# The attention's end and the output projection of layer 1 in program order on TensorE

## The chip, the cores and the metric

The kernel runs on one core of one Trainium2 chip. The metric is the device time of one execution in microseconds (us), the median of several runs, lower is better. The engines are named as the profile names them: PE (TensorE matmul), PEld (its weight load), DVE (VectorE), ACT (ScalarE), POOL (GpSimd), SP (SyncE, which issues transfers).

## The reference

One inference step of a decoder trunk with two layers over 1024 prompt tokens and 8 sample tokens, all in float32, with D_MODEL = 1024 and D_FF = 4096. Layer 0 mixes tokens by a recurrent block, layer 1 by attention with a window of 128 tokens, 16 heads of 64 and 4 KV heads. Each mixer and each MLP is added to the residual stream. The part that matters here is layer 1's mixer; the sample tokens attend to a cache:

```python
def swa_sample(x, k_cache, v_cache, w_qkv, q_g, k_g, sinks, w_out):
    q, k, v = qkv_heads(x, w_qkv, q_g, k_g)
    k_all = jnp.concatenate([k_cache, k], axis=1)
    v_all = jnp.concatenate([v_cache, v], axis=1)
    ...
    o = sink_attention(q, k_all, v_all, dist, mask, sinks)
    y = o.reshape(n, s, Q_DIM) @ w_out
    return y, k_all[:, s:], v_all[:, s:]
```

The prompt's heads go through the same `sink_attention` in blocks of 128, and through the same `w_out`. Behind it follows `h = h + y`, an RMS norm, and the MLP.

## The kernel before

Activations lie as 8 tiles of 128 features by 1032 tokens (1024 of the prompt, then 8 sample tokens). The tokens are cut into 3 chunks c of 344, so the sample tokens stand in chunk 2. A float32 product is made of three: both operands are split into a high and a low part (`oh`, `ol` and `wh`, `wl`), and oh·wh, ol·wh and oh·wl are summed.

**The output projection of layer 1** (`entry_steps`, lines 395 to 430) has a group for each c and each of 8 output tiles m: 8 steps over the features with 3 products 128x344 each, 24 "long products" (line 244). For m < 4 and c < 2, six of the eight steps are done early, while the attention still runs, and the last two later. Behind a group DVE adds the residual tile (L418), ACT issues the write to DRAM (L419), squares (L290) and scales (L421). A generator yields behind every three products, so that the caller can put other work there. When group m = 4 of a chunk is reached (m = 5 for c = 1), `factors` makes the norm's block sums of the chunk before: ACT casts the sum of squares (`shi`, L278), DVE makes the rest (`slo`, L279), and PE multiplies both by ones (L280, L281).

**The attention** runs over 32 steps g. Each has three stages: scores of a step two ahead (`stage_a`, L1033), transposes (`stage_b`, L1060) and values (`stage_c`, L1080, for two steps together). `order` says at which step and in which place of it the scores of step g are written. Between them stand steps of a filler: the query projections up to g = 22 (G0), the early part of the output projection from there on.

**The samples' chain** (`samples`, lines 1115 to 1163) is a generator too: a square on ACT (L1117), a sum over features on PE (L1119), 16 score products of 8 columns (L1131), a copy, a transpose on PE (L1136), a softmax on DVE and ACT (L1138 to L1145), a transpose on PE (L1147), 16 value products of 8 columns (L1154, "short products" as those of L1131), and copies by DVE (L1157, L1163) into the columns that chunk 2 needs. `load_cache` issues its transfers on SP. `between(m, c)` is called ahead of each group, starts both, and asks for weights and residual tiles (`need`).

**The order of the work.** The engines each run their own stream in order. A scheduler makes these streams from the program's order and from estimates. `pinned()` ties the PE instructions inside it to program order, by a dependence from each to the next. The attention's steps stand inside it. The last `stage_c` and the loop that drains the filler, which runs the greater part of the output projection, stand outside:

```python
for _ in fill:
    for s in side:
        next(s, None)
```

Here the scheduler places the samples' products and the block sums among the long products by itself. With each product on 128x128 weights goes a weight load, which PE runs beside the product ahead.

Of the kernel before, what the change touches and what calls it, by code (L numbers as in the profile page):

```python
# [26 lines left out]
NB = SEQ // P  # L27
# [38 lines left out]
def trunk(ctx: ExitStack, tc: tile.TileContext, I, O):  # L66
# [51 lines left out]
    def B(tag=None):  # L118
        if tag is None:
            tag = ring[turn[0] % len(ring)]  # L120
            turn[0] += 1
        return psum["pool"].tile([P, 512], F32, tag=tag, bufs=BANKS[tag], name=nm("b" + tag))
# [71 lines left out]
    for o in [("x", m) for m in range(4)] + LRU:  # L194
        if o[0] == "g":
            units.append(("gate", o[1], I["w_gate"][o[1]], W))
        elif o[0] in "xo":
            m = o[1] + (8 if o[0] == "x" else 0)
# [630 lines left out]
    def attention(hs):  # L829
# [181 lines left out]
        @contextmanager  # L1011
        def pinned():
            block = tc.nc.cur_bb.bb
            n = len(block.instructions)
            yield
            seq = [i for i in block.instructions[n:] if i.engine == pe.engine]
            for x, y in zip(([last["pe"]] if "pe" in last else []) + seq, seq[0 if "pe" in last else 1:]):
                tc.add_manual_dep(y, x.name, mybir.DependencyInfo(mybir.DependencyClass.NoSync, mybir.DependencyReason.DATA), reason="pinned")
            if seq:
                last["pe"] = seq[-1]  # L1020
# [74 lines left out]
        def load_cache():  # L1095
            z = S("z")
            sp.dma_start(z[:, 129:257], I["dist_s"])
            zs.append(z)
            for p in range(2):
                kt = A("kc")  # L1100
                kv = kt[:, :D].rearrange("p (n j) -> p n j", n=NS)
                sp.dma_start(kv[:, :, 0:127], I["k_cache"][p])
                dve.tensor_copy(kv[:, :, 127], ks[:, p, :])
                sp.dma_start(O["ks"][p], kt[:, :D])
                kc.append(kv)
            for h in range(2):
                vt = A("vc")
                vv = vt[:, :D].rearrange("p (n j) -> p n j", n=4)
                for part in (slice(0, 112), slice(112, 127)):
                    sp.dma_start(vv[part], I["v_cache"][part, 4 * h:4 * h + 4, :])  # L1110
                sp.dma_start(vt[127:128, :D], vnew[h:h + 1, :])
                sp.dma_start(O["vs"][h], vt[:, :D])
                vc.append(vv)

        def samples():
            sb = S("ssb")
            act.activation(sb[:, :P], qrow, AF.Square, scale=4.0)  # L1117
            st = B("N")
            pe.matmul(st[:, 0:1], lhsT=sb[:, :P], rhs=ones[:, 0:1], start=True, stop=True)  # L1119
            r = S("r")[:, :1]  # L1120
            rstd_m2(st[:, 0:1], r, 1)
            dve.tensor_scalar(dd[:, 2:3], r, 0.0625, None, ALU.mult)
            dve.reciprocal(dd[:, 3:4], dd[:, 2:3])
            dve.tensor_tensor(dd[:, 3:4], dd[:, 3:4], V("slope_row"), ALU.mult)
            dve.tensor_scalar(qrow, qrow, V("qg"), None, ALU.mult)
            yield
            st = B("N")
            for n in range(NS):
                for p in range(2):
                    o = n * 16 + p * 8  # L1130
                    pe.matmul(st[:, o:o + 8], lhsT=kc[p][:, n, :], rhs=qblk[:, n, p, :, :].rearrange("p u i -> p (u i)"),  # L1131
                              start=True, stop=True)
                    yield
            dve.tensor_copy(sb[:, :P], st[:, :P])
            st2 = B("N")
            pe.transpose(st2[:, :P], sb[:, :P], ident)  # L1136
            z = zs[0]
            dve.tensor_scalar(z[:, 129:257], z[:, 129:257], dd[:, 3:4], -1.0, ALU.mult, ALU.mult)  # L1138
            dve.tensor_copy(z[:, 128:129], nsink_row)
            dve.tensor_tensor_reduce(z[:, 0:P], st2[:, :P], z[:, 129:257], scale=dd[:, 2:3], scalar=nsink_row[:, 0:1],  # L1140
                                     op0=ALU.add, op1=ALU.min, accum_out=dd[:, 0:1])
            e = S("e")
            act.activation(e[:, 0:P + 1], z[:, 0:P + 1], AF.Exp, scale=-1.0, bias=dd[:, 0:1], accum_out=dd[:, 1:2])
            dve.reciprocal(dd[:, 1:2], dd[:, 1:2])
            dve.tensor_scalar(e[:, 0:P], e[:, 0:P], dd[:, 1:2], None, ALU.mult)  # L1145
            st3 = B("N")
            pe.transpose(st3[:, :P], e[:, :P], ident)  # L1147
            dve.tensor_copy(sb[:, P:2 * P], st3[:, :P])
            yield from range(8)
            st4 = B("N")  # L1150
            for n in range(NS):
                for p in range(2):
                    o = n * 16 + p * 8
                    pe.matmul(st4[:, o:o + 8], lhsT=vc[n // 4][:, n % 4, p * P:p * P + P], rhs=sb[:, P + o:P + o + 8],  # L1154
                              start=True, stop=True)
                    yield
            dve.tensor_copy(sb[:, :P], st4[:, :P])  # L1157
            sv = sb[:, :P].rearrange("p (n q u i) -> p n q u i", n=NS, q=2, u=2)
            for t in range(8):
                p, i = divmod(t, 4)  # L1160
                for u in range(2):
                    h = slice(64 * u, 64 * u + 64)
                    dve.tensor_copy(osm[h, t, :], sv[h, :, p, u, i])  # L1163
# [23 lines left out]
        def between(m, c):  # L1187
            if (m, c) == (0, 0):
                swap_banks("po")
            if c < 0 or (m, c) == (4, 0):  # L1190
                need(m + 1)
            if m >= 4 and c == 0:
                need(min(m + 2, M8))
            if (m, c) == (6, 0):
                load_cache()
            if (m, c) == (7, 0):
                side.append(samples())
            if (m, c) == (0, 2):
                for t in range(8):
                    split_act_dve(ohl[t][0], ohl[t][1], osm[:, t, :], slice(SEQ, T))  # L1200

        side = []
        fill = filler()

        NG = 4 * NB
# [5 lines left out]
        def upto(n):  # L1211
            take(n - taken[0])

        def pace(table, g):
            at = max((k for k in table if k <= g), default=min(table))
            to = min((k for k in table if k > g), default=at)
            return table[at] if to == at else table[at] + (table[to] - table[at]) * max(0, g - at) / (to - at)
# [21 lines left out]
        order = {}  # L1239
        for g in range(AHEAD, NG):  # L1240
            at = g - AHEAD
            place = {25: (23, 3), 26: (24, 1)}.get(g) or (at, {0: 3, 1: 1}.get(g % NB, 0))
            order[place] = g

        for g in range(NG):
            table = FILL if g < G0 else EARLY

            def scores(place):
                if (g, place) in order:
                    ready(order[g, place])  # L1250
                    run(stage_a(order[g, place]))

            with pinned():
                scores(0)
                if g != G0:
                    upto(int(pace(table, g + 1 / 3)))
                if g and g % 2 == 0:
                    stage_c(g - 2)
                if g == G0:
                    run(fill)  # L1260
                    taken[0], fill = 0, steps
                scores(1)
                upto(int(pace(table, g + 2 / 3)))
                run(stage_b(g))
                upto(int(pace(table, g + 1)))
                scores(3)
            if g == 17:
                for t in (4, 5):
                    ohl[t] = (A("oh"), A("ol"))
            if g in (20, 21, 23, 24):  # L1270
                ensure(index["wo1", (20, 21, 23, 24).index(g)])
            if g == G0 - 1:
                for t in range(4):
                    load_o(t, cs(0))
                for t in (6, 7):
                    ohl[t] = (A("oh"), A("ol"))
                srcs = [ohl[t] for t in range(8)]
                r1 = A("rt")
                rs["r1"] = r1
                xs, need, steps = out_proj("wo1", srcs, spill, "g_mlp1", r1, spill1, before=between, after=ahead(1),  # L1280
                                          early=(4, 5, 0, 1, 2, 3))
                for t in range(4):
                    load_o(t, cs(1))
            if g == 26:
                for t in range(4):
                    load_o(t, slice(2 * CH, SEQ))
        stage_c(NG - 2)

        for _ in fill:
            for s in side:  # L1290
                next(s, None)
        return xs


# [345 lines left out]
```

## Time and profile before

| | |
|---|---|
| time, median of 3 runs | 1960.44 us (1960.01 to 1960.88) |
| the profiled execution's own time | 1958.56 us |
| its span | 1956.8 us |
| PE busy | 1944.1 us, 99% |
| DVE, ACT, POOL busy | 1480.5, 1007.9, 370.1 us |
| mean granted PE clock | 0.998 |

The span is the time from the first to the last instruction. The profile lists groups of instructions by source line, what each engine waited for, windows of the span with the busy time of each engine and the granted clock, and a timeline. A row of the timeline has the start, the duration, engine, line, operation, output and inputs, and in brackets the idle time ahead of it with what ended it. The long products follow each other closer than their duration says, since they are pipelined: what one costs is the distance from start to start.

### The profile page before, as it was taken

The page shows a single profiled execution, that of the slowest core. Times are in us where ns is not written, and L with a number is a line of the kernel's source. Part 1 is how long each engine was busy: PE and PEld are TensorE (multiplying, and loading weights), DVE is VectorE, ACT ScalarE, POOL GpSimd, SP SyncE. Part 2 cuts the span into 40 slices and gives each one's busy share as a digit, 9 for nine tenths or more (in the row PEclk, how much of TensorE's full clock was granted, in tenths as well). Part 3 has the DMA queues.
Part 4 walks back from the last instruction along what each step waited for, and adds up shares of the span by engine and source line. Part 5 has one row for each costly group of instructions (what it writes and reads, how often), then busy time and mean ns, then how long its engine had stood idle before and what let it go on. Part 6 is the DMA issues. An engine that isn't in the chain of part 4 may idle for free.

```text
span 1956.8 us, 34219 instructions
## 1 busy us (share of the span) xinstructions
PE 1944.1 (99%) x12844; PEld 1808.8 (92%) x12844; DVE 1480.5 (76%) x2712; ACT 1007.9 (52%) x1993; POOL 370.1 (19%) x702
## 2 busy tenths in 40 slices
PE   9999999999999999999999999999999999999998
PEld 8999999999999899999999887999999999999998
DVE  8896737987777888778753778579877779687884
ACT  6476635543434655455553667555443436455552
POOL 2330000000000232322022667000000003223221
PEclk9999999999999999999999999999999999999999
DMA  5111242244445788888453446622443447788876
GB/s 184 44 44 54 67 170 83 109 152 157 141 157 172 232 224 239 215 197 210 135 152 87 111 110 195 212 72 105 157 145 138 162 167 261 212 197 217 237 193 181
DMA packets 115909, 308.17 MB, mean 157 GB/s; under 512 B 17560, under 2 KB 46240, under 8 KB 115744
## 3 DMA queue, kind: packets, MB, share of 16 engines
q0 software_dynamic: 30720, 104.18, 22.0%
q1 hardware_dynamic: 54496, 129.36, 20.1%
q10 hardware_dynamic: 30528, 72.45, 10.3%
q8 instruction: 101, 1.65, 0.4%
q14 instruction: 64, 0.52, 0.1%
HBM read 178.08 MB, written 115.16 MB: 150 GB/s over the span
## 4 chain that ended last, share of the span: by engine, by line
PE 91%; DVE 3%; issue 2%; ACT 2%; DMA 1%; POOL 1%; SPq 0%; ACTq 0%; DVEq 0%; POOLq 0%
PE bD L609 35%; PE bZ L609 26%; PE bP L244 11%; PE bS L244 7%; PE bT L244 3%; PE bP L939 3%; PE bO L1080 1%; PE bSS L1033 1%; PE bS L969 1%; PE bT L1060 1%; ACT se L1046 1%; DMA x<-xT 0%; DVE wl L184 0%; DVE hl L1323 0%; DVE sq L295 0%
## 5 line engine op out<-in xcount | busy, mean ns | idle before, releaser
L609 PEld LDWEIGHTS bD<-op,op 128*128 128x128 f32 x3072 | 380.6, 188 | 7.9
L609 PE MATMUL bD<-op,op 128*128 128x260 f32 x3072 | 383.1, 282 | 0.0
L609 PEld LDWEIGHTS bD<-tl,op 128*128 128x128 f32 x2880 | 362.3, 188 | 11.7 <-DVE ho L757 0.3
L609 PE MATMUL bD<-tl,op 128*128 128x260 f32 x2880 | 366.5, 282 | 0.1
L622 POOL DMA_DIRECT2D tl<-hsum x210 | 125.2, 681 | 889.7 <-PE bD L609 786.5
L456 ACT CAST op<-ws 128x512 fp32r<-128x512 f32 (+2 forms) x288 | 158.6, 560 | 245.5 <-DVE ws L577 119.9
L609 PE MATMUL bZ<-op,op 128*128 128x512 f32 x1152 | 282.3, 395 | 0.0
L609 PE MATMUL bZ<-tl,op 128*128 128x512 f32 x1080 | 271.9, 395 | 1.0 <-ACT he L731 0.8
L609 PEld LDWEIGHTS bZ<-op,op 128*128 128x128 f32 x1152 | 210.4, 188 | 43.8 <-ACT he L743 0.4
L609 PEld LDWEIGHTS bZ<-tl,op 128*128 128x128 f32 x1080 | 194.3, 188 | 38.7 <-ACT he L731 1.0
L464 DVE TENSOR_TENSOR tl<-tl 128x520 fp32r<-128x520 f32 (+1 forms) x210 | 136.7, 692 | 77.2 <-ACT tl L463 77.1
L456 ACT CAST op<-raw 128x512 fp32r<-128x512 f32 (+2 forms) x216 | 120.9, 561 | 135.8 <-PE bD L609 73.6
L457 DVE TENSOR_TENSOR op<-ws,op 128x512 fp32r<-128x512 f32 (+2 forms) x288 | 171.4, 610 | 7.3 <-ACT op L456 7.1
L457 DVE TENSOR_TENSOR op<-raw,op 128x512 fp32r<-128x512 f32 (+2 forms) x216 | 131.6, 610 | 10.6 <-ACT op L456 9.8
L757 DVE TENSOR_TENSOR ho<-bD,ho 128x520 f32<-128x520 f32 x140 | 97.5, 696 | 36.8 <-PE bD L609 35.9
L463 ACT CAST tl<-tl 128x520 fp32r<-128x520 f32 (+1 forms) x210 | 117.7, 626 | 3.0 <-DMA tl<-hsum 1.5
L184 DVE TENSOR_TENSOR wl<-raw,wh 128x512 fp32r<-128x512 f32 (+1 forms) x73 | 63.8, 891 | 34.4 <-ACT wh L183 17.7
L747 DVE TENSOR_TENSOR ho<-bZ,ho 128x512 f32<-128x512 f32 x72 | 49.5, 688 | 43.6 <-PE bZ L609 43.3
L731 ACT COPY he<-bZ 128x512 f32<-128x512 f32 x72 | 42.0, 583 | 74.9 <-PE bZ L609 67.9
L757 DVE TENSOR_TENSOR he<-bD,he 128x520 f32<-128x520 f32 x71 | 49.4, 696 | 40.6 <-PE bD L609 40.3
L749 ACT COPY he<-bZ 128x512 f32<-128x512 f32 x68 | 39.9, 587 | 77.0 <-PE bZ L609 65.0
L183 ACT CAST wh<-raw 128x512 fp32r<-128x512 f32 (+1 forms) x76 | 57.1, 775 | 32.1 <-PE bT L244 11.3
(372 smaller groups left out, 3833.4 us busy)
## 6 DMA issues: line engine op xcount, KB each, us to landing
raw<-w_up SPq DMA_DIRECT2D x64, 512.0 KB, 3.9
tl<-hsum POOLq DMA_DIRECT2D x120, 260.0 KB, 6.8
raw<-w_dn SPq DMA_DIRECT2D x64, 384.0 KB, 6.4
tl<-hsum POOLq DMA_DIRECT2D x90, 256.0 KB, 6.5
spill<-ho POOLq DMA_DIRECT2D x32, 516.0 KB, 6.8
spill<-he POOLq DMA_DIRECT2D x32, 516.0 KB, 6.5
hsum<-ts ACTq DMA_DIRECT2D x30, 520.0 KB, 4.0
hsum<-ho ACTq DMA_DIRECT2D x30, 516.0 KB, 3.6
```

What stands on the lines that cost most here:

```text
L183: act.copy(r_(hi[:, sl]), raw[:, sl])
L184: eng.tensor_tensor(r_(lo[:, sl]), raw[:, sl], hi[:, sl], ALU.subtract)
L244: pe.matmul(o, lhsT=r_(wt[:, col(k):col(k) + P]), rhs=r_(xt[:, cs(c)]), start=(k == first and a == 0), stop=(k == final and a == 2))
L456: act.copy(r_(hi), x)
L457: dve.tensor_tensor(r_(lo), x, hi, ALU.subtract)
L463: act.copy(r_(hi), lo)
L464: eng.tensor_tensor(r_(lo), lo, hi, ALU.subtract)
L609: pe.matmul(d[:, 512 * b:512 * b + c], lhsT=r_(wt[:, j * P:j * P + P]), rhs=r_(xt[:, c * b:c * b + c]), start=first and j == 0 and a == 0, ...
L622: pool.dma_start(t[:, n:2 * n], src)
L747: dve.tensor_tensor(o0, d, o[:, HP], ALU.add)
L757: last["sum"] = dve.tensor_tensor(t, inner(d), t, ALU.add).ins
L939: pe.matmul(o, lhsT=r_(wt[:, k * P:k * P + P]), rhs=r_(xt[:, cs(c)]), start=(k == 0 and a == 0), stop=(k == M8 - 1 and a == 2))
```

## The change

1. The last `stage_c` and the draining loop stand inside `pinned()`. PE so runs the whole output projection of layer 1, with the samples' products and the block sums, in program order.
2. In `samples`, three filler steps are yielded ahead of the first transpose and nine ahead of the second, and three instead of eight ahead of the value products.
3. `load_cache` is called at (m, c) = (3, 0) instead of (6, 0), and `samples` starts at (6, 0) instead of (7, 0). An assertion says that the samples are done when (0, 2) is reached.
4. The scores of steps 17 and 18 get other places in `order`.
5. At g = 22 two steps of the output projection (six long products) stand ahead of `stage_c`, where there were none.

```diff
--- before.py
+++ after.py
@@ -1132,6 +1132,7 @@
                               start=True, stop=True)
                     yield
             dve.tensor_copy(sb[:, :P], st[:, :P])
+            yield from range(3)
             st2 = B("N")
             pe.transpose(st2[:, :P], sb[:, :P], ident)
             z = zs[0]
@@ -1143,10 +1144,11 @@
             act.activation(e[:, 0:P + 1], z[:, 0:P + 1], AF.Exp, scale=-1.0, bias=dd[:, 0:1], accum_out=dd[:, 1:2])
             dve.reciprocal(dd[:, 1:2], dd[:, 1:2])
             dve.tensor_scalar(e[:, 0:P], e[:, 0:P], dd[:, 1:2], None, ALU.mult)
+            yield from range(9)
             st3 = B("N")
             pe.transpose(st3[:, :P], e[:, :P], ident)
             dve.tensor_copy(sb[:, P:2 * P], st3[:, :P])
-            yield from range(8)
+            yield from range(3)
             st4 = B("N")
             for n in range(NS):
                 for p in range(2):
@@ -1191,10 +1193,12 @@
                 need(m + 1)
             if m >= 4 and c == 0:
                 need(min(m + 2, M8))
+            if (m, c) == (3, 0):
+                load_cache()
             if (m, c) == (6, 0):
-                load_cache()
-            if (m, c) == (7, 0):
                 side.append(samples())
+            if (m, c) == (0, 2):
+                assert not any(True for s in side for _ in s)
             if (m, c) == (0, 2):
                 for t in range(8):
                     split_act_dve(ohl[t][0], ohl[t][1], osm[:, t, :], slice(SEQ, T))
@@ -1239,7 +1243,7 @@
         order = {}
         for g in range(AHEAD, NG):
             at = g - AHEAD
-            place = {25: (23, 3), 26: (24, 1)}.get(g) or (at, {0: 3, 1: 1}.get(g % NB, 0))
+            place = {17: (15, 3), 18: (16, 1), 25: (23, 3), 26: (24, 1)}.get(g) or (at, {0: 3, 1: 1}.get(g % NB, 0))
             order[place] = g
 
         for g in range(NG):
@@ -1254,11 +1258,13 @@
                 scores(0)
                 if g != G0:
                     upto(int(pace(table, g + 1 / 3)))
+                if g == G0:
+                    next(steps), next(steps)
                 if g and g % 2 == 0:
                     stage_c(g - 2)
                 if g == G0:
                     run(fill)
-                    taken[0], fill = 0, steps
+                    taken[0], fill = 2, steps
                 scores(1)
                 upto(int(pace(table, g + 2 / 3)))
                 run(stage_b(g))
@@ -1284,11 +1290,11 @@
             if g == 26:
                 for t in range(4):
                     load_o(t, slice(2 * CH, SEQ))
-        stage_c(NG - 2)
-
-        for _ in fill:
-            for s in side:
-                next(s, None)
+        with pinned():
+            stage_c(NG - 2)
+            for _ in fill:
+                for s in side:
+                    next(s, None)
         return xs
```

Lines behind the edits move by 1 to 4: L1136 becomes L1137, L1147 becomes L1149, L1154 becomes L1156. Each product, cast and transfer is there as often as before.

The streams of the engines show what moves. In these rows stand the line, the operation, the output, the inputs and the shape; `bP`, `bS`, `bT` and `bN` are PSUM tiles, and a number after a name tells one tile of that name from another.

**PE, chunk 0.** Before, the samples' sum (L1119) stands behind 16 long products of group m = 7 (`bS_13964`), and six score products follow each other:

```order
L244 MATMUL bS_13964<-oh_12840,wh_13904 128x344
L1119 MATMUL bN_13970<-ones,ssb_13968 128x1
L244 MATMUL bS_13964<-ol_12841,wh_13904 128x344
L244 MATMUL bS_13964<-oh_12840,wl_13905 128x344
L244 MATMUL bS_13964<-oh_13151,wh_13904 128x344
L244 MATMUL bS_13964<-ol_13152,wh_13904 128x344
L244 MATMUL bS_13964<-oh_13151,wl_13905 128x344
L244 MATMUL bS_13964<-oh_13153,wh_13904 128x344
L244 MATMUL bS_13964<-ol_13154,wh_13904 128x344
L1131 MATMUL bN_13987<-st,kc_13914 128x8
L1131 MATMUL bN_13987<-st,kc_13918 128x8
L1131 MATMUL bN_13987<-st,kc_13914 128x8
```

After, it stands behind three products of group m = 6 (`bP_13932`), directly behind those of m = 5 (`bP_13890`), and the score products stand singly:

```order
L244 MATMUL bP_13890<-ol_13154,wh_13840 128x344
L244 MATMUL bP_13890<-oh_13153,wl_13841 128x344
L244 MATMUL bP_13932<-oh_13135,wh_13882 128x344
L244 MATMUL bP_13932<-ol_13136,wh_13882 128x344
L244 MATMUL bP_13932<-oh_13135,wl_13883 128x344
L1119 MATMUL bN_13938<-ones,ssb_13936 128x1
L244 MATMUL bP_13932<-oh_13139,wh_13882 128x344
L244 MATMUL bP_13932<-ol_13140,wh_13882 128x344
L244 MATMUL bP_13932<-oh_13139,wl_13883 128x344
L1131 MATMUL bN_13955<-st,kc_13796 128x8
```

The sum moved forward to three products behind the end of a group. ACT runs L1117, which makes `ssb`, behind the eviction of the group m = 5.

**PE, chunk 1.** Before, the block sums of chunk 0 stand inside group m = 5 (`bS_14143`), behind 16 and 19 of its products, and ten value products follow each other:

```order
L244 MATMUL bS_14143<-oh_12840,wh_13820 128x344
L280 MATMUL bN_14128<-shi_14130,ones 128x344
L244 MATMUL bS_14143<-ol_12841,wh_13820 128x344
L244 MATMUL bS_14143<-oh_12840,wl_13821 128x344
L244 MATMUL bS_14143<-oh_13151,wh_13820 128x344
L281 MATMUL bN_14128<-slo_14131,ones 128x344
```

```order
L244 MATMUL bS_14183<-oh_13143,wl_13863 128x344
L244 MATMUL bS_14183<-oh_13147,wh_13862 128x344
L1154 MATMUL bN_14150<-ssb_13968,vc_13922 128x8 x8
L1154 MATMUL bN_14150<-ssb_13968,vc_13927 128x8 x2
L244 MATMUL bS_14183<-ol_13148,wh_13862 128x344
L244 MATMUL bS_14183<-oh_13147,wl_13863 128x344
```

After, both block sums stand between the last product of m = 4 (`bP_14093`) and the first of m = 5, and the value products stand singly:

```order
L244 MATMUL bP_14093<-oh_13153,wh_13830 128x344
L244 MATMUL bP_14093<-ol_13154,wh_13830 128x344
L244 MATMUL bP_14093<-oh_13153,wl_13831 128x344
L280 MATMUL bN_14128<-shi_14130,ones 128x344
L281 MATMUL bN_14128<-slo_14131,ones 128x344
L244 MATMUL bS_14143<-oh_13135,wh_13840 128x344
L244 MATMUL bS_14143<-ol_13136,wh_13840 128x344
L244 MATMUL bS_14143<-oh_13135,wl_13841 128x344
L1156 MATMUL bN_14147<-ssb_13936,vc_13804 128x8
```

The block sums moved to the border of the two groups, the value products from a batch to every fourth place.

**PE and ACT, chunk 2.** Before, the block sums of chunk 1 stand behind 19 and 23 products of group m = 4 (`bS_14479`):

```order
L244 MATMUL bS_14479<-oh_13151,wh_13810 128x344
L280 MATMUL bN_14464<-shi_14466,ones 128x344
L244 MATMUL bS_14479<-ol_13152,wh_13810 128x344
L244 MATMUL bS_14479<-oh_13151,wl_13811 128x344
L244 MATMUL bS_14479<-oh_13153,wh_13810 128x344
L244 MATMUL bS_14479<-ol_13154,wh_13810 128x344
L281 MATMUL bN_14464<-slo_14467,ones 128x344
L244 MATMUL bS_14479<-oh_13153,wl_13811 128x344
```

After, they stand between m = 3 (`bS_14415`) and m = 4:

```order
L244 MATMUL bS_14415<-ol_13154,wh_13369 128x344
L244 MATMUL bS_14415<-oh_13153,wl_13370 128x344
L280 MATMUL bN_14464<-shi_14466,ones 128x344
L281 MATMUL bN_14464<-slo_14467,ones 128x344
L244 MATMUL bS_14479<-oh_13135,wh_13830 128x344
L244 MATMUL bS_14479<-ol_13136,wh_13830 128x344
```

ACT's stream is the same there in both kernels: the cast that the first block sum needs (`shi_14466`) stands behind the eviction of m = 3 (`y_14440`, which DVE makes from `bS_14415`).

```order
L419 DMA spill_2518<-y_14440 128x344
L290 ACTIVATE sq_14443<-y_14440 128x344
L421 ACTIVATE x_13454<-y_14440,vec 128x344
L278 CAST shi_14466<-sq_14039 128x344
```

Nothing moved on ACT; on PE the block sums moved forward by 19 and 23 long products.

## The prediction

> **What bounds the kernel now.** I read the page first, its busy shares and the chain of waits.
>
> ```profile
> span 1956.8 us, 34219 instructions
> PE 1944.1 (99%) x12844; PEld 1808.8 (92%) x12844; DVE 1480.5 (76%) x2712; ACT 1007.9 (52%) x1993; POOL 370.1 (19%) x702
> PE 91%; DVE 3%; issue 2%; ACT 2%; DMA 1%; POOL 1%; SPq 0%; ACTq 0%; DVEq 0%; POOLq 0%
> ```
>
> TensorE (PE) is busy for 1944.1 of 1956.8 us and carries 91% of the chain that ends last. So a change can save only PE's idle time, PE's slow time or PE's work, and whatever makes PE wait is added to the time almost in full. The change touches attention and the output projection of layer 1. The list of what PE waited for shows three waits of the attention:
>
> ```profile
> PE bO L1080 <- DVE pt L1064: 1.5, 1, 1.5
> PE bSS L1033 <- DVE se L1041: 0.8, 1, 0.8
> PE bSS L1033 <- DVE den L1048: 0.6, 1, 0.6
> ```
>
> (Columns: total us, times, longest.) For slow time I cut the end of the projection into windows of 3.41 us, so that both changes of the clock fall on an edge. Columns: window, length, then busy time and count of PE, weight loads, DVE, ACT, POOL; then the granted clock, the DMA share and GB/s.
>
> ```profile
> 1148.79:1152.20 3.41, 2.56 (x20) 2.28 (x19) 2.33 (x4) 1.29 (x3) 1.38 (x4) 1.00 0.79 235
> 1271.67:1275.08 3.41, 3.41 (x29) 3.41 (x30) 2.50 (x5) 1.61 (x3) 0.00 (x0) 1.00 0.00 0
> 1275.08:1278.49 3.41, 3.41 (x16) 3.41 (x14) 0.16 (x1) 0.00 (x0) 0.00 (x0) 0.50 0.00 0
> 1278.49:1281.91 3.42, 3.42 (x14) 3.42 (x14) 2.20 (x12) 1.75 (x6) 0.00 (x0) 0.50 0.15 54
> 1281.91:1285.32 3.41, 3.41 (x23) 3.41 (x22) 3.20 (x18) 1.31 (x5) 0.00 (x0) 1.00 0.00 0
> ```
>
> The clock is half from 1275.08 to 1281.91 us, 6.83 us, while PE shows itself busy all the time. What stands ahead of it:
>
> ```profile
> 1270.98 0.31 PE L244 MATMUL bS<-oh,wh 128*128 128x344 f32 x1
> 1271.28 2.40 PE L1154 MATMUL bN<-ssb,vc 128*128 128x8 f32 x20
> 1273.53 0.40 PE L244 MATMUL bS<-ol,wh 128*128 128x344 f32 x1
> ```
>
> Ten value products of the sample tokens (20 records), 8 columns wide, stand in one row for 2.25 us. Of the window 1271.67 to 1275.08, they fill 1273.53 − 1271.67 = 1.86 us. I take it that short products hardly count as work: 1.86 us of them in a window cost the clock of the next. An idle stretch of 3.41 − 2.56 = 0.85 us (the first window above) did not.
>
> **The change part by part.**
>
> *The batch goes.* The value products stand singly behind three long ones each. Prices of a group of three long and one short, at full and at half clock, and of a long product at half:
>
> ```profile
> 1258.04 0.28 PE L1131 MATMUL bN<-st,kc 128*128 128x8 f32 x2
> 1258.73 0.28 PE L1131 MATMUL bN<-st,kc 128*128 128x8 f32 x2
> 1276.23 0.49 PE L244 MATMUL bS<-ol,wh 128*128 128x344 f32 x1
> 1276.52 0.49 PE L244 MATMUL bS<-oh,wl 128*128 128x344 f32 x1
> 1276.81 0.43 PE L1154 MATMUL bN<-ssb,vc 128*128 128x8 f32 x2
> 1278.09 0.43 PE L1154 MATMUL bN<-ssb,vc 128*128 128x8 f32 x2
> ```
>
> A group takes 1258.73 − 1258.04 = 0.69 us at full and 1278.09 − 1276.81 = 1.28 us at half clock; a long product takes 0.29 us at half and 0.157 us at full clock (1249.61 to 1251.81 below, 14 steps). A single short one costs 0.69 − 3 × 0.157 = 0.22 us, one of the batch 2.25 / 10 = 0.225 us, so singling them is free. The gap ahead of the batch (1270.98 + 0.16 to 1271.28, 0.14 us) goes. If the throttle goes too, that saves 6.83 × (1 − 0.157 / 0.29) = 3.1 us.
>
> *The attention.* Two groups of places move and two steps of the projection are put ahead of a `stage_c` that waited. Of the waits of 1.5, 0.8 and 0.6 us, two steps are six long products, 6 × 0.157 = 0.94 us, which cover 0.94 of the 1.5; the moved scores steps can take most of the 0.8. But products used early are missing later, and the wait of 0.6 us comes after. Between 0.3 and 2.9 us saved; I take 1.2, since the third wait ends on DVE, which gets no faster.
>
> *Program order on PE.* This is where I expect the loss. Before, the scheduler put short products where their inputs were ready. Now each stands where it is written. I follow three, each by the rows of before for the same chain, since ACT's and DVE's order around them is the one of before.
>
> First, the samples' sum of squares (L1119) now stands three long products behind the last of group m = 5, c = 0. Its input is made on ACT by L1117, queued behind that group's own eviction. The rows of the group before it now:
>
> ```profile
> 1249.61 0.32 PE L244 MATMUL bP<-oh,wl 128*128 128x344 f32 x1
> 1249.97 0.52 DVE L418 TENSOR_TENSOR y<-bP,x 128x344 f32<-128x344 f32 x1 [1.28 <-PE bP L244]
> 1250.89 0.49 ACT L290 ACTIVATE sq<-y 128x344 f32<-128x344 f32 x1 [2.28 <-DVE y L418]
> 1251.29 0.57 ACT L421 ACTIVATE x<-y,vec 128x344 f32<-128x344 f32 x1
> 1251.76 0.29 ACT L1117 ACTIVATE ssb<-st 128x128 f32<-128x128 f32 x1
> 1251.81 0.32 PE L244 MATMUL bS<-ol,wh 128*128 128x344 f32 x1
> 1252.30 0.28 PE L1119 MATMUL bN<-ones,ssb 128*128 128x1 f32 x2
> ```
>
> From the start of the last product (1249.61) to L1117's end (1252.05) are 2.44 us. L1119 would be reached after four steps, 0.63 us. PE stands for 2.44 − 0.63 = 1.8 us, with the semaphore 2.0. Before, sixteen long products of the next group ran in that time. Everything on PE is queued behind L1119; ACT and DVE, who would evict the next group, wait for PE.
>
> Second, the block sums of c = 0 (L280, L281) now stand directly between group m = 4 and m = 5 of c = 1. ACT's cast L278 is still behind the eviction of m = 4:
>
> ```profile
> 1265.00 0.32 PE L244 MATMUL bP<-oh,wl 128*128 128x344 f32 x1
> 1266.73 0.57 ACT L421 ACTIVATE x<-y,vec 128x344 f32<-128x344 f32 x1
> 1267.20 0.46 ACT L278 CAST shi<-sq 128x344 fp32r<-128x344 f32 x1
> 1267.70 0.52 DVE L279 TENSOR_TENSOR slo<-sq,shi 128x344 fp32r<-128x344 f32 x1 [0.23 <-ACT shi L278]
> ```
>
> L281 would be reached two steps behind 1265.00, at 1265.31; its input is ready at 1268.22: 2.9 us.
>
> Third, the same for c = 1, between m = 3 and m = 4 of c = 2:
>
> ```profile
> 1299.03 0.32 PE L244 MATMUL bS<-oh,wl 128*128 128x344 f32 x1
> 1299.22 1.14 ACT L456 CAST op<-x 128x512 fp32r<-128x512 f32 x2 [1.74 <-PE bS L244]
> 1300.70 0.57 ACT L421 ACTIVATE x<-y,vec 128x344 f32<-128x344 f32 x1
> 1301.18 0.47 ACT L278 CAST shi<-sq 128x344 fp32r<-128x344 f32 x1
> 1301.52 0.69 DVE L490 TENSOR_TENSOR x<-x,x 128x520 f32<-128x520 f32 x1
> 1302.13 0.51 DVE L279 TENSOR_TENSOR slo<-sq,shi 128x344 fp32r<-128x344 f32 x1
> ```
>
> L281 reached at 1299.34, ready at 1302.64: 3.3 us. Without DVE's L490 in between it is 2.8 (L278 ends at 1301.65, with 0.51 of L279 1302.16); I take 3.2.
>
> The transposes get three and nine steps ahead of them, 3 × 0.47 and 9 × 0.47 us; their chains are covered, and I price them at nothing. The cover is long products that must run anyway. At the end, after the last value product, only 24 long products (3.8 us) remain before c = 2 needs the samples' columns:
>
> ```profile
> 1279.84 0.29 DVE L1157 COPY ssb<-bN 128x128 f32<-128x128 f32 x1 [1.00 <-PE bN L1154]
> 1283.61 0.71 DVE L272 TENSOR_TENSOR ol<-st,oh 128x8 fp32r<-128x8 f32 x8
> ```
>
> That chain lasts 1284.32 − 1279.84 = 4.5 us, of which the first columns are needed at its start: 0 to 0.7, I take 0.4.
>
> *The caches* are loaded from (3,0) on and so stand ahead of residual tiles and weights in SP's queue. If those come late, the first stall grows; I put 0 to 2 us on it, and nothing in the sum, since the projection's tiles were issued early before.
>
> *Sum without the clock:* −3.1 − 0.1 − 1.2 + 2.0 + 2.9 + 3.2 + 0.4 = +4.1 us.
>
> *The clock.* Each stall is an empty stretch longer than the 0.85 us that was forgiven, two of them longer than the 1.86 us that was not. What counts is how much falls in one window of 3.41 us. For a stall of 2.9 us a window holds 1.86 or more in (0.51 + 2 × 1.04) / 3.41 = 76% of the positions, for 3.2 us in 85%, for 2.0 us in 49%. A throttle of one window costs 3.41 × 0.46 = 1.55 us. After the third only long products follow: 1.55. After the first and second sixteen singles follow, and in the trace singles did not bring the clock back at once, so two windows, 3.1. At worst the clock stays half through all sixteen: 16 × (1.28 − 0.69) = 9.4 us each. Likeliest: the second and the third throttle, the first doesn't: +3.1 + 1.55 = +4.65 us. Bounds: 0 and 9.4 + 9.4 + 1.55 = 20.
>
> Here the Trainium skill speaks against me. Its page "TensorE: Matmul & The Clock Gate", section "HAM oscillation — how this bites in real kernels", gives the rule that PE must not idle for more than about 3.4 us at a stretch. By it none of my three stalls costs the clock. The trace disagrees in one point: its throttle came with PE busy throughout. With the rule the sum stays at +4.1; it is the first rival below.
>
> **Forecast.** The profiled execution took 1958.56 us, 1.76 more than its span; +4.1 + 4.65 makes 1967.3. The timed runs of before have a median 1.9 us higher (1960.44), so a timed run may be 1969; half of that difference can be a throttle's phase, which changes here anyway. I say 1967.5 us.
>
> **Rivals.**
> 1. *The stalls don't cost the clock.* For it: no idle gap in this trace was ever followed by half clock; against it, 1.86 us of short products was enough. Time 1958.56 + 4.1 = 1962.7, against the median 1964.5: within 0.2%, barely.
> 2. *Faster: the stalls are covered.* One mechanism: ACT's chain ends so early that L278 and L1117 are done when PE reaches them. It decides if L278's distance from the group's last product falls below two steps, 0.3 us, where it is 2.2 us now. Then the change does what its words say: 1958.56 − 3.1 − 0.1 − 1.2 + 0.4 = 1954.6, timed 1956.5 at most. Against it: ACT's order is unchanged there.
> 3. *The clock stays half through the singles.* For it: in the window from 1275.08, with two groups of singles in it, the clock did not come back. Two such stretches: 1958.56 + 4.1 + 9.4 to 20 = 1972 to 1983.
> 4. *The change of places does nothing, and caches come late:* no 1.2 saved, 2 more on the first stall, 1962.7 + 3.2 = 1966, with the clock up to 1971. On my forecast's side.
>
> **How the numbers follow.** Chances: forecast 0.46, rival 1 0.21, rival 2 0.12, rival 3 0.12, rival 4 0.09. The likeliest one's own range is 1964 to 1971. This kernel's change can be told from none beyond 0.2%, 3.9 us: 1956.5 to 1964.4. Faster: most of rival 2, 0.11. Same: most of rival 1 and the low edge of the forecast, 0.25. Slower: the rest, 0.64. The range runs from 1960 (leaving out rival 2 and a little of rival 1) to 1976 (leaving out half of rival 3).
>
> **What would show it.** In the changed profile: no run of L1156 records longer than one; no half clock that follows L1156 as a batch. L1119 preceded by some 2.0 us idle put down to ACT's L1117; L280 or L281 twice preceded by 2.9 and 3.2 us put down to ACT's L278 or DVE's L279. Windows with clock 0.5 right after the second and third of these. The waits of L1080 and L1033 smaller by about 1.2 us in all. I am wrong if PE's list of waits does not hold L1119, L280 and L281 with at least 6 us, or if PE idles there and the clock stays at 1.00.

## The result and the profile after

The changed kernel takes 1988.6 us (median of four runs, 1976.63 to 1993.84) against 1960.39 us (1960.01 to 1960.88): a ratio of 1.0135 with a 95% interval of 1.0089 to 1.0182. It is slower, by 28 us. Its profiled execution has a span of 1985.2 us, 28.4 us more than before.

Where the time went is seen when the span is cut into stages at the same instructions: the first score product, the last product of `stage_c`, the first product of the MLP. Of the windows view of the kernel before, the attention and the drained projection (columns: window, length, busy time and count of PE, PEld, DVE, ACT, POOL, then granted clock, DMA share, GB/s):

```profile
1059.40:1234.00 174.60, 170.80 (x1236) 147.73 (x1236) 128.42 (x305) 119.31 (x401) 112.25 (x306) 1.00 0.50 146
1234.00:1314.60 80.60, 80.60 (x510) 79.54 (x507) 52.98 (x131) 41.15 (x92) 0.00 (x0) 0.96 0.36 119
```

and of the changed kernel:

```profile
1059.86:1236.80 176.94, 171.46 (x1236) 147.65 (x1236) 128.19 (x306) 118.88 (x401) 111.69 (x306) 1.00 0.49 145
1236.80:1342.63 105.83, 94.41 (x510) 91.81 (x507) 53.92 (x132) 40.66 (x92) 0.00 (x0) 0.84 0.26 89
```

The same 510 records of the projection take 105.83 us instead of 80.60, 25.2 us more. The attention takes 2.3 us more. What lies before and behind these stages adds the last 0.9 us. In the projection two things are new: PE is idle for 105.83 − 94.41 = 11.4 us where it was never idle, and the mean clock is 0.84 instead of 0.96.

The idle time stands in the list of what PE waited for (total us, times, longest):

```profile
PE bN L280 <- ACT shi L278: 5.0, 2, 2.6
PE bN L1119 <- ACT ssb L1117: 3.1, 1, 3.1
PE bN L1156 <- DVE q L313: 1.8, 1, 1.8
PE bSS L1033 <- DVE se L1041: 1.7, 2, 1.6
PE bSS L1033 <- DVE den L1048: 1.6, 1, 1.6
...
PE bN L893 <- ACT sq L877: 1.1, 1, 1.1
...
PE bN L281 <- DVE slo L279: 0.5, 1, 0.5
PE bO L1080 <- DVE pt L1064: 0.5, 2, 0.3
PE bN L1131 <- DVE q L313: 0.5, 1, 0.5
...
PE bP L244 <- DVE ol L272: 0.3, 1, 0.3
```

Six of these rows are the projection's (L280, L1119, L1156, L281, L1131 and L244), the other four the attention's. The clock is told by windows that begin and end where it changes, to 0.05 us:

```profile
1247.80:1251.21 3.41, 1.59 (x10) 1.30 (x9) 0.79 (x2) 0.93 (x2) 0.00 (x0) 1.00 0.99 380
1251.22:1254.63 3.41, 1.59 (x9) 1.31 (x10) 2.40 (x9) 1.93 (x7) 0.00 (x0) 1.00 0.89 332
1254.63:1258.04 3.41, 3.41 (x16) 3.41 (x15) 0.37 (x2) 0.00 (x0) 0.00 (x0) 0.51 0.26 98
1268.29:1271.70 3.41, 3.41 (x15) 3.41 (x14) 0.00 (x0) 0.00 (x0) 0.00 (x0) 0.50 0.00 0
1271.70:1275.11 3.41, 3.41 (x25) 3.39 (x24) 2.04 (x5) 1.88 (x4) 0.00 (x0) 0.99 0.27 99
1281.93:1285.35 3.42, 1.31 (x5) 0.79 (x5) 0.96 (x3) 2.29 (x6) 0.00 (x0) 1.00 0.03 8
1295.59:1299.00 3.41, 3.41 (x13) 3.41 (x14) 1.45 (x3) 1.58 (x3) 0.00 (x0) 0.50 0.14 52
1322.90:1326.31 3.41, 1.03 (x5) 0.80 (x6) 2.75 (x6) 1.91 (x5) 0.00 (x0) 1.00 0.14 52
1326.31:1329.72 3.41, 3.41 (x14) 3.41 (x13) 1.09 (x2) 1.43 (x3) 0.00 (x0) 0.51 0.00 0
```

Half clock begins three times, each time behind a window in which PE stood idle for 1.8 to 2.4 us (3.41 less its busy time): from 1254.63 to 1271.70 (five windows of 3.41 us), from 1285.35 to 1299.00 (four), and from 1326.31 to 1329.72 (one). The first window of the list has 1.8 us of idle time too and kept the clock; the last section comes back to that. PE worked for 10 × 3.41 − 0.6 = 33.5 us at half clock (0.6 us of them it stood idle behind 1285.35). At the prediction's pitches of a long product, 0.157 and 0.29 us, that cost 33.5 × (1 − 0.157 / 0.29) = 15.4 us; before there were two windows, 3.1 us. So of the projection's 25.2 us, 11.4 are idle time, 12.3 are clock; 1.5 are left over.

### The profile page after: what moved, and what is told of

It is laid out like the page before. It is cut to its first block, busy times and chain, and to the rows that moved or that the text cites. A ratio compares the mean times of both kernels' runs of the same rounds, so it can differ in the third digit from the quotient of the medians.

```text
span 1985.2 us, 34209 instructions
## 1 busy us (share of the span) xinstructions
PE 1958.8 (99%) x12844; PEld 1820.8 (92%) x12844; DVE 1479.5 (75%) x2712; ACT 1006.6 (51%) x1993; POOL 368.4 (19%) x702
## 4 chain that ended last, share of the span: by engine, by line
PE 88%; DVE 4%; DMA 3%; issue 2%; ACT 2%; POOL 0%; SPq 0%; ACTq 0%; DVEq 0%; POOLq 0%
PE bD L609 34%; PE bZ L609 25%; PE bP L244 11%; PE bS L244 7%; PE bT L244 3%; PE bP L939 3%; PE bS L969 1%; PE bSS L1033 1%; PE bO L1080 1%; DMA raw<-w_out 1%; ACT se L1046 1%; DMA x<-xT 1%; PE bT L1060 0%; DVE wl L184 0%; DVE sq L295 0%
## 5 line engine op out<-in xcount | busy, mean ns | idle before, releaser
L464 DVE TENSOR_TENSOR tl<-tl 128x520 fp32r<-128x520 f32 (+1 forms) x210 | 136.4, 691 | 76.8 <-ACT tl L463 76.6
```

Of the source, the lines that this page charges most:

```text
L464: eng.tensor_tensor(r_(lo), lo, hi, ALU.subtract)
```

## The experiments

In `d_early` and the kernels built on it, lines behind 278 stand up to 16 further down (L1048 is 1033 before, L1095 is 1080, L1135 the samples' sum, L1147 their score products, L1172 the value products, L284 and L285 the block sums).

**Which edit does it.** One kernel undoes the pinning alone, one makes it alone.

```diff
# a_unpinned: the changed kernel with
-        with pinned():
-            stage_c(NG - 2)
-            for _ in fill:
+        stage_c(NG - 2)
+        for _ in fill:
# b_pin_only: the kernel before, with the opposite of this
```

> The changed kernel with the last stage_c and the draining loop outside pinned() again; all other edits stay. Theory P (program order makes the stalls, and the stalls cost the clock): PE's waits on L119, L280, L281 and the first value product go, half clock falls to the two windows of before or none, and what is left is the attention's own loss of 1.7 us; 1958 to 1963 us. Theory Q (another edit does it: the caches loaded early, or the steps moved in the attention): the time stays above 1975 us. By L119 the sum at line 1119 is meant.

> The kernel before with this one edit: last stage_c and draining loop inside pinned(). Theory P: program order alone makes stalls, and here also one of about 3 us ahead of the second transpose (no steps are put ahead of it); half clock of 6 windows or more; 1975 to 1995 us. Theory Q: 1958 to 1963 us.

Measured: `a_unpinned` 1965.18 us (1959.88 to 1971.75), ratio 1.0035 (1.0018 to 1.0052); `b_pin_only` 1991.3 us (1984.64 to 1993.27), ratio 1.0173 (1.0156 to 1.0190). The kernel before had a median of 1958.68 beside them. Pinning alone costs as much as the whole change (the two intervals overlap), and without it most of the loss is gone, so theory P holds. But the unpinned kernel lies above the 1963 us I gave as upper bound, by its median and in five of its eight executions: in its profile the sum at L1119 waits 1.0 us, six score products follow as a batch, and then the clock is half for four windows (1256 to 1270 us), and for a fifth behind a batch of value products (1287 to 1290 us). The waits of `b_pin_only`:

```profile
PE bN L280 <- ACT shi L278: 4.7, 2, 2.4
PE bN L1147 <- DVE e L1145: 2.5, 1, 2.5
PE bN L1119 <- ACT ssb L1117: 1.7, 1, 1.7
```

The second is the transpose ahead of which the change puts nine filler steps, and which does not wait there: that part of the change does what I priced it at.

**Stalls or short products.** `d_early` keeps program order and the single short products, but has the inputs of the stalled products made earlier:

```diff
+                if early and m == 3 and stats:
+                    stats[-1][0].ahead()        # cast shi, rest slo
                 if m == (5 if early and c == 1 else 4) and stats:
-                    factors(stats.pop(), B("N"))
+                    factors(stats.pop(), B("O" if early else "N"))
...
-            if (m, c) == (6, 0):
+            if (m, c) == (5, 0):
                 side.append(samples())
...
             act.activation(sb[:, :P], qrow, AF.Square, scale=4.0)
+            yield from range(8)
...
-            yield
+            yield from range(2)             # ahead of the score products
```

> The changed kernel, program order kept, with the inputs of the stalled products made earlier: ACT's cast and DVE's rest for the block sums are written at m = 3, one or two groups ahead of the products; the block sums get a PSUM bank of their own; the samples start at (5, 0), and eight filler steps stand between their square on ACT and their sum on PE. The short products stay single, one behind every three long ones. Theory S (the stalls cost the clock, the singles only hold it down once it is lost): no PE wait over 0.5 us in the projection, no half clock there, 1988 - 11 of stalls - 15 of clock = 1956 to 1962 us. Rival T (singles alone, one in four, lose the clock): 5 or more windows of half clock stay, 1968 us or more.

Measured: 1965.59 us, scattered from 1958.78 to 1974.36; ratio 1.0034 (1.0017 to 1.0051). Neither expectation holds for all executions. The profiled one (1960.96 us) has clock 1.00 in the projection, with all its single short products, as theory S says. In five of the ten the mean clock is 0.993 to 0.995, and their times are those that the rival gives. What was left standing there:

```profile
PE bSS L1048 <- DVE den L1063: 3.3, 2, 1.8
...
PE bN L1147 <- DVE q L326: 1.2, 1, 1.2
```

A wait of 1.2 us ahead of the first score product was still there, and the attention waited longer than before. Two further kernels take these away. `f_early_old_att` takes `d_early` and undoes the edits in the attention; `g_early_more` in addition lets the samples start at (4, 0) and puts four steps more ahead of the score products:

```diff
-            if (m, c) == (5, 0):
+            if (m, c) == (4, 0):
                 side.append(samples())
...
-            yield from range(2)
+            yield from range(6)
             st = B("N")
```

> The kernel of d_early with the attention of before: the scores of steps 17 and 18 in their old places, no projection steps ahead of stage_c at g = 22. Theory A (the moved steps ask for the projection's weights earlier, ACT's casts of them stand ahead of the softmax and wait for the transfer): from the first scores to the last stage_c 174.5 us as before, against 176.8 in the changed kernel less 0.9 us of projection work; 2 us faster than d_early in undisturbed clock, span 1955 to 1957 us. Rival: the attention's part stays at 176 us, since the caches loaded early do it. The wait of 1.2 us ahead of the first score product stays, and if that and the singles together cost the clock, half clock of 4 to 7 windows comes in some of the executions (times up to 1970).

> The kernel of f_early_old_att with the samples started at (4, 0) and five steps more ahead of the first score product, so that it need not wait. Theory S (an empty stretch is needed to lose the clock, the singles only hold it down): no PE wait over 0.3 us in the projection, clock 1.00 in it, 1955 to 1957 us in every execution, faster than before by some 2 us. Rival T (singles, one in four, lose the clock by themselves when they fall well into the windows): executions scatter up to 1970 us as those of d_early did.

(The last says five steps where four were added.) Measured: `f_early_old_att` 1959.52 us (1956.46 to 1971.82), ratio 1.0021 (1.0006 to 1.0035); `g_early_more` 1956.08 us (1953.48 to 1958.60), ratio 0.9990 (0.9981 to 0.9999), with 1958.64 for the kernel before. The attention of `f_early_old_att`, from the first score product to the last `stage_c`, takes 174.3 us in its profile, that of `d_early` 178.3; both load the caches early, so the rival that the caches lengthen it falls. Five of its twelve executions still lose the clock (mean 0.994 to 0.997). In the profiled one the score products waited 2.3 us, and this followed:

```profile
1247.78:1251.20 3.42, 1.14 (x9) 0.92 (x7) 2.73 (x9) 2.14 (x7) 0.00 (x0) 0.99 1.03 412
1251.20:1254.61 3.41, 3.41 (x16) 3.41 (x14) 0.13 (x1) 0.00 (x0) 0.00 (x0) 0.50 0.45 177
1254.61:1258.02 3.41, 3.41 (x15) 3.41 (x15) 0.67 (x2) 0.68 (x2) 0.00 (x0) 0.50 0.06 21
1258.02:1261.44 3.42, 3.42 (x15) 3.42 (x14) 0.36 (x1) 0.29 (x1) 0.00 (x0) 0.51 0.09 31
```

In `g_early_more`, without this wait, the two stretches from the first to the last short product:

```profile
1247.17:1257.60 10.43, 10.43 (x77) 10.43 (x76) 3.54 (x8) 3.07 (x6) 0.00 (x0) 1.00 0.62 238
1265.13:1275.87 10.74, 10.74 (x78) 10.74 (x78) 4.05 (x9) 5.00 (x11) 0.00 (x0) 1.00 0.14 51
```

PE is busy and the clock full over three windows each, and the mean clock of its eleven executions is 0.999 or 1.0. One short product behind every three long ones does not lose the clock; rival T falls. That the half clocks of `d_early` came from its wait of 1.2 us was not seen in a trace of it, where the clock held behind that wait; it is inferred from `f_early_old_att`, which has the wait and the loss, and from `g_early_more`, which lacks both.

**What holds the clock down.** `e_half_short` keeps the stalls of the changed kernel and leaves out every second short product, so that the samples' output is no longer that of the reference:

```diff
-                for p in range(2):
-                    o = n * 16 + p * 8
-                    pe.matmul(st[:, o:o + 8], lhsT=kc[p][:, n, :], ...)
-                    yield
+                o = n * 16
+                pe.matmul(st[:, o:o + 16], lhsT=kc[0][:, n, :], ...)
+                yield
+                yield
# and the same for the value products
```

> The changed kernel with half of the samples' score and value products left out (each of the eight left is 16 columns wide, for one pair of heads; the samples' output is not that of the reference), one behind every six long products instead of every three. The stalls ahead stay as they are. Theory S (a mix of one short to three long is too thin to bring the clock back at half speed): the half clock after the first and second stall ends after one or two windows instead of five and four, 8 x 0.22 x 2 = 3.5 us of short products go, and the time is 1970 to 1980 us. Rival (the length of a throttle is set by the stall, not by what follows): again four and five windows, 1982 to 1990 us.

Measured: 1971.98 us (1968.20 to 1974.96), ratio 1.0070 (1.0054 to 1.0086). The clock, right behind the first and the second stall:

```profile
1249.91:1253.32 3.41, 3.41 (x17) 3.41 (x16) 0.56 (x3) 0.00 (x0) 0.00 (x0) 0.60 0.56 222
1253.32:1256.73 3.41, 3.41 (x22) 3.41 (x23) 0.93 (x2) 0.94 (x2) 0.00 (x0) 0.90 0.14 46
...
1271.00:1274.41 3.41, 1.89 (x8) 1.45 (x7) 1.60 (x3) 2.55 (x5) 0.00 (x0) 0.51 0.00 0
1274.41:1277.82 3.41, 3.41 (x14) 3.41 (x13) 0.70 (x2) 0.00 (x0) 0.00 (x0) 0.50 0.00 0
1277.82:1281.23 3.41, 3.41 (x24) 3.41 (x24) 1.12 (x2) 0.92 (x2) 0.00 (x0) 0.98 0.02 5
```

One window after the first stall (the first two rows share it) and two after the second, instead of five and four. The first stall, 1.7 us, is shorter than the changed kernel's 3.1, so it proves less; the second, 2.6 us and 1.5 at the first value product, is much the same there (2.6 and 1.8). So what follows a stall has a large part in how long a throttle lasts. `k_one_stall` turns this round: `g_early_more` with only the last stall put back, and nothing but long products behind it.

```diff
-                if early and m == 3 and stats:
+                if early and m == 3 and c == 1 and stats:
                     stats[-1][0].ahead()
```

> The kernel of g_early_more with one stall put back: for chunk 2 the cast and the rest for the block sums stand directly ahead of their products again, as in the changed kernel. Behind the stall only long products follow. Theory S: PE waits 2.4 and 0.5 us there; the clock is lost for one window of 3.41 us in most executions, 1.55 us, and comes back since long products alone are dense enough: 1956.1 + 3.1 + 1.0 to 1.6 = 1960 to 1961 us, scatter of no more than 3 us. Rival (a stall throttles for long whatever follows): 1965 us or more.

Measured: 1961.83 us (1959.94 to 1963.24), ratio 1.0014 (1.0005 to 1.0024). That is 5.75 us over `g_early_more` (measured in another session, in which the kernel before was 0.2 us slower), a little above the 4 to 5 expected; the scatter stays at 3.3 us, and the half clock lasts one window, 1300.7 to 1304.1 us of the span. One late cast and its rest cost this kernel 5.75 us, of which 2.9 are the waits

```profile
PE bO L284 <- ACT shi L278: 2.3, 1, 2.3
...
PE bO L285 <- DVE slo L279: 0.6, 1, 0.6
```

and 1.55 the clock. The rest, 1.3 us, is partly a wait of 0.8 us at L1135, which `g_early_more` does not have. (In the profiled executions the projection alone, 1234.27 to 1316.77 us, is 82.5 us long against 76.6.)

**The attention.** Its two edits were put apart onto `g_early_more`: `h_places` has the new places, `i_steps` the two projection steps ahead of `stage_c`.

```diff
# h_places
-            place = {25: (23, 3), 26: (24, 1)}.get(g) or ...
+            place = {17: (15, 3), 18: (16, 1), 25: (23, 3), 26: (24, 1)}.get(g) or ...
# i_steps
+                if g == G0:
+                    next(steps), next(steps)
                 if g and g % 2 == 0:
                     stage_c(g - 2)
...
-                    taken[0], fill = 0, steps
+                    taken[0], fill = 2, steps
```

> The kernel of g_early_more with the scores of steps 17 and 18 in their new places. Theory A (the moved projection steps cost, the places alone do not): the wait of 0.9 us at line 1048 (1033 before) goes, a wait of 1.1 us for the query norm comes near it: 0 to 1 us either way, 1955 to 1957 us. Rival: these places bring the late weights too, waits of 1.5 us behind 1195 us of the span, 1957 to 1960 us.

> The kernel of g_early_more with the two projection steps ahead of stage_c at g = 22. Theory A: the wait of 1.5 us ahead of line 1095 (1080 before) shrinks to 0.2, and two waits of about 1.5 us come behind 1195 us of the span, where ACT waits for the projection's weights with the softmax queued behind: 1956 to 1959 us. Rival: the 1.3 us stay gained, 1954 to 1955 us.

Measured, beside 1958.82 us for the kernel before: `h_places` 1959.19 us (1957.76 to 1961.38), ratio 1.0001 (0.9992 to 1.0010); `i_steps` 1954.74 us (1953.85 to 1956.61), ratio 0.9980 (0.9971 to 0.9989). Theory A had them the wrong way round; both kernels came out in the range of its rival. Against `g_early_more` the places cost 3.1 us, and the median with the steps is 1.3 us lower. The stage from the first score product to the last `stage_c`, for `g_early_more`, `h_places` and `i_steps`:

```profile
1059.51:1235.21 175.70, 170.67 (x1235) 147.68 (x1235) 128.18 (x305) 119.23 (x401) 111.23 (x306) 1.00 0.50 145
```

```profile
1059.92:1238.27 178.35, 171.94 (x1235) 147.43 (x1235) 127.79 (x305) 118.81 (x401) 111.95 (x306) 1.00 0.48 143
```

```profile
1058.80:1233.23 174.43, 170.77 (x1234) 147.63 (x1234) 128.33 (x305) 119.13 (x401) 111.61 (x306) 1.00 0.50 147
```

With the places PE is idle for 6.4 us instead of 5.0, and busy for 1.3 us more with the same products; why, no run shows. The gain by the steps is not shown by this stage: `k_one_stall`, with the attention of `g_early_more`, takes 174.0 us there (1059.70 to 1233.74), less than `i_steps`. One execution of the same attention differs from another by up to 1.7 us. Two waits of `h_places` are longer or new:

```profile
PE bO L1095 <- DVE pt L1079: 2.8, 3, 1.5
...
PE bN L908 <- ACT sq L892: 1.1, 1, 1.1
```

The second is a query norm's sum that the moved scores leave less time for. `i_steps` is faster than the kernel before, by 4.1 us of medians, and than the changed one: program order on PE pays a little when nothing stands late in it.

## Why the prediction was wrong

**The direction and the three stalls held; the clock, as the largest term, was sized at less than a third, and the attention had the wrong sign.** I forecast +8.9 us on the profiled execution's time and a range up to 1976; it became 28.4 us. By its steps:

- *The batch goes, singling is free*: held. In `g_early_more` the short products stand singly and PE loses neither idle time nor clock; from the first product behind `stage_c` to the MLP it takes 76.6 us (1235.74 to 1312.35) against 80.2 before (1234.48 to 1314.65), 3.6 us less where I had 3.2.
- *The three stalls*, 2.0 + 2.9 + 3.2 us: placed right, each on the instruction and the releaser named. Measured 3.15, 2.62 + 0.14 and 2.40 + 0.52. The first is larger because L1117 was queued behind more than the eviction:

```profile
1250.28 0.62 ACT L183 CAST wh<-raw 128x512 fp32r<-128x512 f32 x1 [2.61 <-DMA raw<-w_out]
...
1252.19 0.29 ACT L1117 ACTIVATE ssb<-st 128x128 f32<-128x128 f32 x1
```

 ACT stood 2.61 us for a weight transfer; this is the late transfer on which I put 0 to 2 us and took nothing. All nine kernels that load the caches early have ACT stand so for `w_out`, for 1.2 to 3.1 us; the kernel before and `b_pin_only`, which load them later, do not, and the first stall of `b_pin_only` is 1.7 us. No run moves the caches alone.
- *A stall I did not see.* The first value product waits 1.82 us for DVE's L313, and the first score product 0.49 us for the same line. Both write a PSUM tile `bN`, of which there is one bank, and L313 still reads a sum in it: the block sums' ahead of the value product, the samples' own ahead of the score product. I followed the data of each pinned product, not its PSUM bank. `d_early` gives the block sums another bank and earlier inputs, and the wait of the value product is gone; the samples' sum stays in `bN`, and so does the wait of the score product. In all, idle time came to 11.4 us where the sum had 8.5.
- *The clock*: the term that failed. My sum had three windows, 4.65 us (the second and the third stall throttle, the first not); measured were ten, 15.4 us. All three stalls throttled, and behind the first two the clock stayed half through fourteen and ten of the sixteen single short products. That was the third rival, with a chance of 0.12 and 9.4 us for each stretch; by its time, 1972 to 1983 us, it fell short as well. Its evidence stood in the quoted windows: the one from 1275.08, with short products standing singly, had not brought the clock back. I took that to last two windows, where it could last as long as the mix. The spread of the timed runs, 17 us, goes with their mean clock: 0.995 at 1976.63 us, 0.988 at 1993.84.
- *The attention*, −1.2 us: wrong in sign, +2.3 us. The wait of 1.5 us went, as forecast (L1080 now 0.5 in all). I took the moved scores to be free cover; alone they cost 3.1 us. In the changed kernel ACT also stands for weights, with the softmax queued behind:

```profile
1194.13 1.14 ACT L183 CAST wh<-raw 128x512 fp32r<-128x512 f32 x2 [2.56 <-DMA raw<-w_out]
1200.85 1.14 ACT L183 CAST wh<-raw 128x512 fp32r<-128x512 f32 x2 [1.99 <-DMA raw<-w_out]
```

 The kernel before has 0.6 us of this, `i_steps` 0.8, `h_places` 1.3, while `d_early`, with both edits, has 2.7 and 1.9. So such long waits come from both edits together; but `a_unpinned`, with both too, has 1.3 and 0.9, and no run shows what else sets them.
- *The samples' columns for chunk 2*, 0.4 us: 0.27 us at L244. Held.

Against the sum, the measured terms are +2.9 (idle), +10.75 (clock), +3.5 (attention) and some 2.4 in what is left: 1.5 us in the projection and 0.9 outside these stages. That PE starts again slowly behind each of eight waits, some 0.2 us each, would make up the 1.5; it was not measured by itself.

The rule of the Trainium skill that I weighed, "TensorE: Matmul & The Clock Gate", section "HAM oscillation — how this bites in real kernels" (PE must not idle for more than about 3.4 us), would have kept the clock here. The trace disagrees: no idle stretch was longer than 3.15 us, and three windows of 3.41 us with 1.8, 2.1 and 2.4 us of idle time were each followed by half clock. The first rival, built on it, falls.

## What to carry to other kernels

Fixing the order on an engine turns every late input in that order into a stall of the whole engine; before doing it, follow for each short instruction what makes its input, what is queued ahead of that maker on its own engine, and whether its PSUM bank is free. Here two casts written a group earlier, one more bank and an earlier start turned a loss of 28 us into a small gain (1954.7 against 1958.8 us, with the new places left out). A stall's price is its length plus the clock that it loses, and how long the clock stays lost is set by the work behind it: don't put thin work behind a place where PE may wait.

## What the runs showed of the hardware

I had priced idle time. It does not sort the windows: in the changed kernel that from 1247.80 and that from 1251.22 both have 1.8 us of it, and only behind the second was the clock lost. How much long work starts in a window sorts them better. Counted from the timelines, on windows that end at the clock's own changes (some 0.05 us behind the edges above), the products of 344 columns that start in 3.41 us:

| window | long products | the clock behind it |
|---|---|---|
| before, 1271.67 (the batch, PE shown busy throughout) | 7 | lost |
| changed, 1251.27, 1281.99 and 1322.95 (the stalls) | 6, 5, 5 | lost |
| `e_half_short`, 1247.20 and 1267.68; `f_early_old_att`, 1247.74; `k_one_stall`, 1297.24 | 9, 3; 3; 6 | lost |
| `b_pin_only`, 1249.84, 1273.73 and 1321.52; `a_unpinned`, 1252.78 and 1283.50 | 3, 6, 4; 8, 9 | lost |
| changed, 1247.86 and 1278.58 (where a stall begins); `e_half_short`, 1301.82; `b_pin_only`, 1266.91 | 8, 7; 9; 9 | kept |
| changed, at half clock, one short to three long | 7, 8, 9, 7, 8; 6, 8, 8, 8 | stays half seven times, comes back twice (behind the last of each row) |
| before, 1275.08 and 1278.49, at half clock | 8, 10 | stays half, comes back |
| `f_early_old_att`, at half clock | 8, 8, 8 | stays half twice, comes back |
| `e_half_short`, at half clock, one short to six long | 9; 4, 10 | comes back; stays half, comes back |
| changed, 1326.36; `k_one_stall`, 1300.65 (only long ones) | 12, 12 | comes back |

Six and fewer always lost the clock or left it low, ten and more always kept or brought it back, and seven to nine went both ways (a few records may be missing, so each count is good to one or so). So the count is not the whole rule; the short products, for one, are not in it. But it fits that the same mix did both. A group of three long and one short takes 0.69 us at full clock, 3 × 3.41 / 0.69 = 15 long products in a window, and `g_early_more` ran it at clock 1.00. At half clock it takes 1.29 us, 8 in a window, among the counts that went both ways, and the clock stayed low for five and four windows. In the kernel before, singles at half clock had the same 8 in the window from 1275.08. In every trace the clock changed at distances of whole windows, some 1.55 us of loss each. The scatter of the kernel before fits that, 1955.2 us at a mean clock of 1.000 to 1964.5 at 0.996 over 27 runs; only one of its executions was seen in a trace.
